# Two transformer blocks: zero matmuls in the plan's gaps, an early table for ScalarE, a new model of the DMA limits and new offsets

## The chip, the cores and the metric

The kernel runs on one core of a Trainium2 chip. The time is device microseconds of one execution; the number given is the median of the runs. TensorE (PE) multiplies, and its weight loads are listed apart (PEld); VectorE (DVE), ScalarE (ACT) and GpSimd (POOL) do the rest; SyncE (SP) only issues DMAs.

## What is computed

256 tokens of width 1024 go through two blocks of two layers each. In every layer of the first block there is a feed-forward (ffn1), a mixer of a bidirectional gated DeltaNet and a Hyena of order 2 (mix1), and a second feed-forward (ffn2). In every layer of the second block there is a mixer of differential attention, retention and a short convolution with gates (mix2), and a feed-forward with a convolution (ffn3). Cut to its frame:

```python
def _swiglu(h, w_gate, w_up, w_down):
    return (jax.nn.silu(h @ w_gate) * (h @ w_up)) @ w_down
for i in range(DEPTH):                                   # first block
    x = x + 0.5 * _swiglu(_rmsnorm(x, ffn1_norm[i]), ...)
    proj = _rmsnorm(x, mix_norm[i]) @ w_in[i]
    x = x + concatenate([o_dn, o_hy], axis=-1) @ w_out[i]   # DeltaNet, Hyena
    x = x + 0.5 * _swiglu(_rmsnorm(x, ffn2_norm[i]), ...)
# Hyena, after a short convolution of u into v, x1, x2
zz = v
for o, gate in enumerate((x1, x2)):
    zz = gate * (_fft_conv(zz, kspec[:, o]) + skip[o] * zz)
# second block, per layer
x = x + (gate0 * (o_da @ w_da) + gate1 * (o_ret @ w_ret) + gate2 * (o_sc @ w_sc)) @ w_out
x = x + (silu(conv(g_ff)) * u_ff) @ w_ffn_out
```

Inputs and outputs are fp32, and the result has to hold to fp32 accuracy.

## The kernel before

**Weights.** All weights come as 604 chunks of 128x1024 fp32 (512 KB), in the order of use, through SP's DMA queue into four buffers `ws`. ScalarE copies each into `wh` (rounded to fp32r, four buffers), and VectorE, sometimes POOL, makes the rest `wl = ws - wh`. The activations are split in the same way. One product is three fp32r matmuls (`mm3`, L689): high by high, low by high, high by low. A chunk of 128x1024 takes 24 matmuls of 128x256. Results gather in PSUM, three banks `mm` (tile names `pmm_...`) and five `acc` (`pacc_...`). What is left in fp32 (transposes, token sums by `cst`, the doubling in the DeltaNet's solver) is multiplied as fp32. In the names, `c_...` is an activation or constant in SBUF, `sm_...` a narrow one, `par` and `cst` the parameters and constants, `ds` and `dv` buffers in DRAM.

**The plan.** The kernel doesn't issue its instructions as they are written. Class `Plan` records every call as an operation with engine, cost, predecessors and tiles (`note`, L396), places all of them on a simulated clock (`place`, L447) and emits them in the order of the planned starts (`emit`, L616; every instruction has the line of `emit`, L621). So each engine's queue is in the order that the plan gives, and the engines wait for each other by semaphores. `place` takes, on an engine that is free, the ready operation of the highest rank; the rank is the length of the work behind it (times `SLACK` outside TensorE's main chain), and the table `AHEAD` adds an offset by kind and part ("mix1 hyena", "sq0"). Operations that may run on VectorE or POOL (`et`, L701) go by the table `POOL`: of a name's operations every n-th goes to POOL. DMAs are held back while the planned bus is more than `BACK` us ahead. After a gap, TensorE's next group is charged up to 1.7 us more for a slow clock.

**The start.** `setup` (L942) issues on ScalarE's queue the four parts of x and `cst`, then `par`; other constants (`hyf`, `feats`, `cdec`, `oh`, `relb`) follow on the same queue from the parts that need them, and the plan mixes them with ScalarE's copies. While ScalarE's next instruction is a DMA that can't be issued yet, the copies behind it wait. ScalarE's function table is loaded ahead of its first activation.

**mix1.** Beside the projections' main chain, side parts run: the DeltaNet's convolution, solver and scan, and `hyena` (L1578). For each of its two orders: sums and differences `c` with transposes, four products with `zmat` (128x512), eight products of the results with the filter's spectrum on VectorE, then `imat` matmuls and the multiplication by the gate (`hg`, may go to POOL).

## Time and profile before

| | us |
|---|---|
| median of the runs | 1942.88 (1941.55 to 1950.27, three runs) |
| the profiled execution | 1946.58 |
| its span, first to last instruction | 1944.9 |
| TensorE busy | 1910.2 (98%) |
| VectorE busy | 1509.2 (78%) |
| ScalarE busy | 1090.5 (56%) |
| POOL busy | 213.1 (11%) |
| mean granted clock of TensorE | 0.994 |

Busy times count instructions, not waits. A busy TensorE can still be slow: at the lower of its two clock levels (1.2 instead of 2.4 GHz, a granted clock of 0.50) a matmul takes about twice as long, so the clock of a stretch is read beside its busy time. "Idle before <-X" names what an instruction waited for. A time stands at the start of a row in us from the start of the span.

### The profile page before, as it was taken

Reading aid. Unit: us, or ns where it says so; the run is one execution under the profiler, and the core shown is the slowest. Engines: PE = TensorE matmul, PEld = TensorE weight load, DVE = VectorE, ACT = ScalarE, POOL = GpSimd, SP = SyncE. Lnnn points to the kernel's source line nnn. Section 1 sums busy time; section 2 is a strip of 40 time slices with the busy share of each in tenths; the row PEclk is TensorE's granted clock in tenths of the full one; section 3 lists DMA queues with packets and bytes.
Section 4 is the critical chain, followed back from the end, with each engine's and each line's share of the span. In section 5 each row is a group of like instructions: output and inputs, shape, how many; then the busy total and the mean of one; then the engine's idle time right before and its main releaser. Section 6 shows DMA issues by size and latency. Waiting matters only on the chain.

```text
span 1944.9 us, 36536 instructions
## 1 busy us (share of the span) xinstructions
PE 1910.2 (98%) x14038; PEld 1800.6 (93%) x14038; DVE 1509.2 (78%) x3067; ACT 1090.5 (56%) x1792; POOL 213.1 (11%) x218
## 2 busy tenths in 40 slices
PE   7999998999999999999999999999999999999999
PEld 7998997999999999998999999999999999999998
DVE  7768879986669667899886679766977788669776
ACT  5656664565556555664555565455655654556564
POOL 0000041000000000222000002233000012240000
PEclk9999998999999999999999999999999999999999
DMA  8655763255555556552565544555555544555553
GB/s 293 212 185 170 230 195 103 91 197 189 184 186 178 189 186 217 201 149 85 166 195 186 189 167 163 180 185 187 183 186 192 174 153 161 191 182 191 188 185 130
DMA packets 127046, 348.84 MB, mean 179 GB/s; under 512 B 24758, under 2 KB 39960, under 8 KB 126872
## 3 DMA queue, kind: packets, MB, share of 16 engines
q1 hardware_dynamic: 115584, 326.89, 51.3%
q10 hardware_dynamic: 11288, 19.63, 2.9%
q8 instruction: 110, 1.80, 0.4%
q14 instruction: 64, 0.52, 0.1%
HBM read 333.61 MB, written 11.81 MB: 178 GB/s over the span
## 4 chain that ended last, share of the span: by engine, by line
PE 91%; DVE 5%; ACT 1%; DMA 1%; issue 1%; ACTq 0%; POOL 0%; SPq 0%; DVEq 0%; POOLq 0%
PE pmm L621 57%; PE pacc L621 35%; DVE c L621 4%; DVE wl L621 1%; ACT c L621 1%; ACTq L621 0%; ACT wh L621 0%; DVE sm L621 0%; DVE x L621 0%; DMA ds<-c 0%; DMA c<-dv 0%; DMA ws<-in_W 0%; DMA x<-in_x 0%; POOL c L621 0%; ACT L621 0%
## 5 line engine op out<-in xcount | busy, mean ns | idle before, releaser
L621 PE MATMUL pmm<-c,wh 128*128 128x256 f32 (+1 forms) x4576 | 1102.4, 322 | 9.9 <-ACT wh L621 8.6
L621 ACT ACTIVATE wh<-ws 128x1024 fp32r<-128x1024 f32 (+1 forms) x604 | 635.6, 1055 | 537.0 <-PE pmm L621 221.3
L621 DVE TENSOR_TENSOR wl<-ws,wh 128x1024 fp32r<-128x1024 f32 (+1 forms) x562 | 687.7, 1226 | 270.9 <-ACT wh L621 265.0
L621 PE MATMUL pmm<-c,wl 128*128 128x256 f32 x3056 | 859.6, 281 | 0.1
L621 PEld LDWEIGHTS pmm<-c,wh 128*128 128x128 f32 x4576 | 759.8, 189 | 81.1 <-ACT wh L621 8.6
L621 PEld LDWEIGHTS pmm<-c,wl 128*128 128x128 f32 x3056 | 577.6, 189 | 1.0 <-DVE wl L621 0.6
L621 PE MATMUL pacc<-c,wh 128*128 128x256 f32 x3136 | 566.9, 281 | 0.0
L621 PEld LDWEIGHTS pacc<-c,wh 128*128 128x128 f32 x3136 | 482.6, 189 | 6.1 <-issue 0.7
L621 PE MATMUL pacc<-c,wl 128*128 128x256 f32 x1568 | 440.5, 281 | 0.0
L621 PEld LDWEIGHTS pacc<-c,wl 128*128 128x128 f32 x1568 | 296.0, 189 | 0.0
L621 ACT ACTIVATE c<-c 128x256 fp32r<-128x256 f32 (+4 forms) x412 | 181.2, 450 | 157.2 <-DVE c L621 144.3
L621 DVE TENSOR_TENSOR c<-c,c 128x256 f32<-128x256 f32 (+7 forms) x345 | 166.9, 497 | 7.9 <-ACT c L621 4.4
L621 DVE TENSOR_TENSOR c<-pmm,c 128x256 f32<-128x256 f32 (+1 forms) x292 | 134.5, 461 | 41.9 <-PE pmm L621 36.0
L621 DVE SCALAR_TENSOR_TENSOR c<-c,c 128x256 f32<-128x256 f32 (+3 forms) x288 | 129.3, 450 | 14.3 <-ACT c L621 7.7
L621 POOL TENSOR_TENSOR wl<-ws,wh 128x1024 fp32r<-128x1024 f32 x42 | 104.2, 2480 | 263.3 <-ACT wh L621 145.0
L621 DVE SCALAR_TENSOR_TENSOR c<-c,par,c 128x256 f32<-128x256 f32 x248 | 114.7, 482 | 22.9 <-ACT c L621 21.7
L621 PE MATMUL pacc<-c,c 128*128 128x128 f32 (+5 forms) x700 | 98.9, 302 | 2.8 <-DVE c L621 1.4
L621 ACT ACTIVATE c<-pacc 128x512 f32<-128x512 f32 (+4 forms) x125 | 59.2, 495 | 64.3 <-PE pacc L621 60.2
L621 POOL TENSOR_TENSOR c<-c,c 128x256 f32<-128x256 f32 (+1 forms) x50 | 60.9, 1222 | 291.6 <-DVE c L621 245.5
L621 PEld LDWEIGHTS pacc<-c,c 128*128 128x128 f32 (+2 forms) x700 | 83.1, 195 | 8.9 <-DVE c L621 2.3
L621 ACT ACTIVATE c<-c,par 128x256 f32<-128x256 f32 x96 | 52.8, 574 | 51.0 <-DVE c L621 50.4
L621 DVE TENSOR_TENSOR c<-pacc,c 128x512 f32<-128x512 f32 (+4 forms) x126 | 72.0, 610 | 9.3 <-PE pacc L621 6.6
(85 smaller groups left out, 997.6 us busy)
## 6 DMA issues: line engine op xcount, KB each, us to landing
ws<-in_W SPq DMA_DIRECT2D x600, 512.0 KB, 3.4
ds<-c ACTq DMA_DIRECT2D x20, 256.0 KB, 4.7
c<-ds ACTq DMA_DIRECT2D x20, 256.0 KB, 3.8
c<-dv SPq DMA_DIRECT2D x32, 128.0 KB, 2.7
dv<-c SPq DMA_DIRECT2D x8, 256.0 KB, 5.0
dg<-c SPq DMA_DIRECT2D x8, 256.0 KB, 3.2
c<-in_cm ACTq DMA_DIRECT2D x6, 256.0 KB, 5.0
ws<-in_W SPq DMA_DIRECT2D x4, 256.0 KB, 6.4
```

Source lines behind the costliest of these rows:

```text
L621: getattr(e, call)(*a, **kw)
```

## The change

Five things change in the plan, and the order of all queues with them.

1. `AHEAD` (the offsets) is new as a whole, `POOL` (what POOL takes) in nine places, `BACK` is 3.0 instead of 5.
2. The plan's limits for DMAs: 330 instead of 360 KB per us; a DMA waits for the end of the eighth before it (`lanes`); a DMA that follows a DMA, issued by ScalarE, is planned 6.5 us after it; an issue holds ScalarE for 0.35 us.
3. A gap on TensorE is charged with up to 0.3 us, not 1.7 (`COLD`).
4. `emit` puts matmuls of zeros into TensorE's queue where the plan has it waiting for more than 0.45 us (`FILL`). They write into the PSUM tile of the group that follows; the group's first matmul starts the tile anew. At the very start they begin at the planned 3.5 us. POOL makes the zeros in `setup`, by a memset and a copy to fp32r.
5. `setup` gives ScalarE a Tanh on two columns, so that the table is loaded early.

There are 74 zero matmuls: 22 of 128x256 ahead of the first real one, 13 of 128x256 soon after, in layer 0 of mix1 four of 128x512, 13 of 128x1 and one of 128x128 in fp32, in layer 1 six of 128x512 and six of 128x128 in fp32, and nine of 128x256 in four other places. ScalarE loads its table 11 times instead of 13.

Between VectorE and POOL: in layer 0 of mix1 two weight subtractions and one `hg` product go from POOL to VectorE, in layer 1 two subtractions, in mix2 eight; 17 other operations go the other way, among them four elementwise products of mix1 and ffn and nine weight subtractions of mix2 and ffn3.

```diff
-BACK = 5
-AHEAD = {' cst': -57, ' prep': 0, ' sq0': 25, ' x0': 82, 'conv': 5, ...
+BACK = 3.0
+AHEAD = {' ': 42.0, ' cst': 51.0, ' prep': -105.0, ' sq0': 391.0, ' table': -150.0, ...
+COLD, FILL = .3, .45
-POOL = {'ba': 1, 'by': 1, 'gate': 4, 'hg': 3, 'ht': 2, 'hx0': 2, 'hx1': 4, 'hx3': 2, 'mask': 1, 'rot': 4, 'rvg': 1, 'sc': 2, 'sc1': 6, 'se': 4, 'v1': 6, 'wo2': 2}
+POOL = {'ba': 4, 'by': 1, 'daq': 4, 'gate': 6, 'hg': 6, 'ht': 2, 'hx0': 2, 'hx1': 4, 'mask': 1, 'rot': 4, 'rqk': 3, 'rvg': 1, 'sc': 2, 'se': 4, 'sh': 4, 'sq': 6, 'wo2': 2}
...
-            return out.shape[0] * n * 4 / 360e3 * (1.0 if n > 300 else 1.6)
+            return out.shape[0] * n * 4 / 330e3 * (1.0 if n > 300 else 1.6)
...
-            return .95
+            return 6.5 if b.dma and b.eng == "ACT" else .95
...
-        hw = bus = 0.0
+        hw, bus = 0.0, 3.0
+        lanes = [0.0] * 8
...
-                    if ops[i].dma and bus > t + BACK:
+                    if ops[i].dma and max(bus - BACK, lanes[-8]) > t:
...
-                    now[e] = t + .06 if e != "POOL" else t + 1.1
+                    now[e] = t + (.06 if e == "SP" else .35)
...
+                    lanes.append(bus + .2)
...
-                        c += 1.7 * min(max(t - now[e] - 1.1, 0.0) / 2.2, 1.0)
+                        c += COLD * min(max(t - now[e] - 1.1, 0.0) / 2.2, 1.0)
...
+        end, pitch = 3.5, .2
...
+            if o.eng == "PE":
+                if o.start - end > FILL:
+                    self.keep_busy(o.calls[0], o.start - end - .2, pitch)
+                end, pitch = o.end, .118
...
+    def keep_busy(self, first, us, pitch):
+
+        call, a, kw = first
+        out = a[0]
+        n = int(np.prod(out.shape[1:]))
+        fast = call == "matmul" and kw["rhs"].dtype == F32R
+        z = self.zero if fast else self.zero32
+        z, w = z[:, 0:n], z[:, 0:out.shape[0]]
+        if len(out.shape) == 3:
+            z = z.rearrange("p (a b) -> p a b", a=out.shape[1])
+        start = True if call == "transpose" else kw["start"]
+        for _ in range(int(us / (pitch * max(1.0, n / (256 if fast else 64))))):
+            self.real["PE"].matmul(out, lhsT=w, rhs=z, start=start, stop=False, skip_group_check=True)
...
+        nc.zero = fix.tile([128, 512], F32R, name="zero")
+        nc.zero32 = fix.tile([128, 512], F32, name="zero32")
+        nc.gpsimd.memset(nc.zero32, 0.0)
+        nc.gpsimd.tensor_copy(out=nc.zero, in_=nc.zero32)
...
-        nc.part = ""
+        nc.part, nc.hold = "table", .35
+        z = self.T("sm", [128, 2, 2])
+        nc.vector.memset(z[:, 0], 0.0)
+        self.act(z[:, 1], z[:, 0], AF.Tanh)
+        nc.part, nc.hold = "", 0.0
```

At three places the order of an engine's queue is shown. In the names the last number counts the kernel's tiles and moves by two or three from before to after, so `wh_127` of before is `wh_130` of after. ScalarE at the start, before, from the split of the first weights to the copy `wh_127`:

```order
L621 ACTIVATE wh_102<-ws_101 128x512
L621 ACTIVATE wh_105<-ws_104 128x512
L621 DMA c_71_154<-in_hyf 64x256
L621 DMA c_70_153<-in_feats 33x256
L621 DMA c_142_225<-in_hyf 128x512
L621 DMA c_134_217<-in_cdec 128x512
L621 DMA c_135_218<-in_cdec 128x512
L621 DMA c_246_330<-in_hyf 128x512
L621 DMA par<-in_par 128x1764
L621 ACTIVATE wh_127<-ws_126 128x1024
L621 DMA c_210_293<-in_oh 32x256
```

And after, over the same work:

```order
L631 ACTIVATE wh_123<-ws_122 128x1024
L631 ACTIVATE wh_105<-ws_104 128x512
L631 ACTIVATE wh_108<-ws_107 128x512
L631 ACTIVATE c_12_92<-x 128x256
L631 ACTIVATE c_13_93<-x 128x256
L631 DMA c_72_157<-in_hyf 64x256
L631 ACTIVATE wh_130<-ws_129 128x1024
L631 DMA c_71_156<-in_feats 33x256
L631 DMA c_143_228<-in_hyf 128x512
L631 DMA par<-in_par 128x1764
L631 ACTIVATE wh_143<-ws_142 128x1024
```

The copy (now `wh_130`) has come ahead of the DMAs of `feats`, `hyf` and `par`, and `cdec`, one `hyf`, `oh` and `relb` have gone further back; `cst`, which was issued in front of all activations, stands three rows above the first one shown.

TensorE in layer 0 of mix1, before: the last transforms by `zmat`, a sum by `cst`, a product of the filter (64x256) and the `imat` matmuls (128x129) of the Hyena; `pacc_824` is the DeltaNet's doubling in fp32:

```order
L621 MATMUL pacc_904<-c_787_871,zmat 128x512
L621 MATMUL pacc_904<-c_788_872,zmat 128x512
L621 MATMUL pacc_904<-c_787_871,zmat 128x512
L621 MATMUL pacc_900<-cst,c_802_886 128x1 x4
L621 MATMUL pacc_1083<-c_981_1065,c_982_1066 64x256
L621 MATMUL pacc_940<-imat,c_802_886 128x129
L621 MATMUL pacc_940<-imat,c_845_929 128x129
L621 MATMUL pacc_940<-imat,c_812_896 128x128
L621 MATMUL pacc_940<-imat,c_843_927 128x128
L621 MATMUL pacc_940<-imat,c_802_886 128x129
L621 MATMUL pacc_940<-imat,c_845_929 128x129
L621 MATMUL pacc_824<-c_700_784,c_660_744 128x2x4x16 x2
```

And after, with the zeros (L645):

```order
L631 MATMUL pacc_883<-c_788_874,zmat 128x512
L631 MATMUL pacc_883<-c_789_875,zmat 128x512
L631 MATMUL pacc_883<-c_788_874,zmat 128x512
L645 MATMUL pacc_907<-zero 128x512
L631 MATMUL pacc_907<-c_788_874,zmat 128x512
L631 MATMUL pacc_907<-c_789_875,zmat 128x512
L631 MATMUL pacc_907<-c_788_874,zmat 128x512
L645 MATMUL pacc_903<-zero_80 128x1 x13
L631 MATMUL pacc_903<-cst,c_803_889 128x1 x4
L631 MATMUL pacc_1086<-c_982_1068,c_983_1069 64x256
L645 MATMUL pacc_827<-zero_80 128x2x4x16
L631 MATMUL pacc_827<-c_701_787,c_661_747 128x2x4x16 x2
```

The doubling (now `pacc_827`) stands ahead of the `imat` matmuls, and 15 zero matmuls fill three gaps here (three more are a few rows earlier).

VectorE in layer 1 of mix1, before: from the second to the fourth product of the Hyena's transforms with the spectrum (`c_2119`, `c_2128`, and then `c_2129`), with the DeltaNet's convolution (`c_1966`, `c_2010`) and weight subtractions (`wl`) between:

```order
L621 TENSOR_TENSOR c_2119_2203<-pacc_2196,c_2116_2200 128x512
L621 SCALAR_TENSOR_TENSOR c_1966_2050<-c_1961_2045,par,c_1966_2050 128x256
L621 TENSOR_TENSOR c_1955_2039<-pacc_2038,c_1925_2009 128x512
L621 TENSOR_TENSOR c_1951_2035<-pacc_2034,c_1898_1982 128x512
L621 SCALAR_TENSOR_TENSOR c_1966_2050<-c_1961_2045,par,c_1966_2050 128x256
L621 SCALAR_TENSOR_TENSOR c_2010_2094<-c_2004_2088,par,c_2010_2094 128x256 x2
L621 SCALAR_TENSOR_TENSOR sm_1993<-sm_1991,sm_1990 128x8
L621 SCALAR_TENSOR_TENSOR c_1966_2050<-c_1967_2051,c_1966_2050 128x512
L621 TENSOR_TENSOR wl_2211<-ws_2209,wh_2210 128x1024
L621 SCALAR_TENSOR_TENSOR c_2010_2094<-c_2011_2095,c_2010_2094 128x512
L621 TENSOR_TENSOR c_2128_2212<-pacc_2193,c_2116_2200 128x512
L621 TENSOR_TENSOR wl_2240<-ws_2238,wh_2239 128x1024
```

And after, from the first of the eight products (`c_2119` here) to the last:

```order
L631 TENSOR_TENSOR c_2119_2205<-pacc_2196,c_2116_2202 128x512
L631 TENSOR_TENSOR c_2120_2206<-pacc_2199,c_2117_2203 128x512
L631 TENSOR_TENSOR c_2129_2215<-pacc_2196,c_2117_2203 128x512
L631 TENSOR_TENSOR c_2130_2216<-pacc_2199,c_2118_2204 128x512
L631 TENSOR_TENSOR c_2160_2246<-pacc_2223,c_2158_2244 128x512
L631 TENSOR_TENSOR c_2161_2247<-pacc_2240,c_2159_2245 128x512
L631 TENSOR_TENSOR c_2162_2248<-pacc_2223,c_2159_2245 128x512
L631 TENSOR_TENSOR c_2163_2249<-pacc_2240,c_2158_2244 128x512
```

The eight products now stand in a row, and the convolution and two weight subtractions have moved behind them.

## Rows read from the trace of the kernel before

**Rows 1.** The page, part 1: engine, busy us (share of the span), instructions.

```profile
PE 1910.2 (98%) x14038; PEld 1800.6 (93%) x14038; DVE 1509.2 (78%) x3067; ACT 1090.5 (56%) x1792; POOL 213.1 (11%) x218
```

**Rows 2.** Windows, long: from:to, length, busy us (x instructions) by engine, clock, DMA share, GB/s.

```profile
350.00:780.00 430.00, 429.73 (x3053) 401.49 (x3052) 324.61 (x588) 237.66 (x380) 11.82 (x13) 1.00 0.55 183
1050.00:1900.00 850.00, 848.74 (x6382) 806.28 (x6381) 646.95 (x1290) 476.63 (x776) 126.35 (x109) 1.00 0.54 180
```

**Rows 3.** Windows of the start.

```profile
8.60:15.00 6.40, 6.30 (x26) 5.76 (x27) 6.37 (x12) 6.40 (x13) 0.00 (x0) 1.00 0.78 281
15.00:20.80 5.80, 5.80 (x51) 5.80 (x51) 2.42 (x6) 1.07 (x2) 0.00 (x0) 1.00 1.02 375
20.80:24.10 3.30, 0.30 (x4) 0.09 (x2) 2.99 (x14) 2.21 (x3) 0.00 (x0) 1.00 1.02 394
24.10:28.60 4.50, 4.50 (x26) 4.50 (x27) 4.21 (x9) 2.82 (x7) 0.94 (x1) 0.62 0.94 313
```

**Rows 4.** Timeline of ScalarE (ACTq issues DMAs): start, length, what, [idle before <-releaser].

```profile
5.28 1.28 ACT L621 ACT_TABLE_LOAD   x1 [5.28 <-DMA x<-in_x]
6.58 1.43 ACT L621 ACTIVATE c<-x 128x512 f32<-128x512 f32 x3
...
14.39 0.62 ACT L621 ACTIVATE wh<-ws 128x512 fp32r<-128x512 f32 x1
18.33 0.33 ACTq L621 DMA_DIRECT2D c<-in_hyf  x1
...
19.20 1.06 ACT L621 ACTIVATE wh<-ws 128x1024 fp32r<-128x1024 f32 x1 [4.19 <-DMA ws<-in_W]
```

**Rows 5.** Timeline of VectorE at the start.

```profile
20.29 1.23 DVE L621 TENSOR_TENSOR wl<-ws,wh 128x1024 fp32r<-128x1024 f32 x1 [3.38 <-ACT wh L621]
...
23.89 0.15 DVE L621 SCALAR_TENSOR_TENSOR sm<-sm,sm 128x2 f32<-128x2 f32 x1
```

**Rows 6.** Timeline of TensorE, at the start and in layer 0 of mix1.

```profile
15.56 0.50 PE L621 MATMUL pacc<-cst,c 128*128 128x1 f32 x4
...
24.10 0.43 PE L621 MATMUL pacc<-cst,sm 128*128 128x128 f32 x2 [3.00 <-DVE sm L621]
...
309.83 1.41 PE L621 MATMUL pacc<-c,zmat 128*128 128x512 f32 x5 [1.23 <-DVE c L621]
```

**Rows 7.** Windows around 220 and 250 us, and of both layers of mix1.

```profile
219.80:223.20 3.40, 3.40 (x18) 3.40 (x17) 3.40 (x13) 0.63 (x1) 0.00 (x0) 0.50 0.48 161
240.00:260.00 20.00, 17.16 (x135) 16.18 (x134) 15.84 (x47) 10.76 (x18) 7.10 (x10) 1.00 0.73 238
303.70:311.90 8.20, 5.16 (x31) 3.57 (x30) 8.15 (x23) 4.36 (x10) 0.00 (x0) 1.00 0.21 25
311.90:318.80 6.90, 3.97 (x12) 2.33 (x12) 6.37 (x11) 0.48 (x2) 2.55 (x2) 0.75 0.75 201
318.80:325.60 6.80, 5.44 (x25) 5.45 (x26) 5.44 (x10) 4.15 (x8) 0.71 (x2) 0.50 0.67 200
...
868.00:875.00 7.00, 5.12 (x37) 4.19 (x35) 6.96 (x19) 5.23 (x13) 0.00 (x0) 1.00 0.31 35
875.00:878.50 3.50, 3.20 (x8) 2.53 (x9) 3.37 (x6) 0.00 (x0) 0.00 (x0) 0.52 0.71 185
878.50:892.00 13.50, 10.36 (x79) 9.16 (x78) 11.95 (x22) 7.66 (x17) 6.45 (x6) 1.00 0.75 228
...
919.50:923.00 3.50, 3.42 (x16) 3.42 (x17) 3.50 (x9) 1.23 (x2) 0.91 (x2) 0.51 0.14 23
```

**Rows 8.** VectorE's groups from 868 to 892: count, busy us, mean ns, idle before.

```profile
L621 DVE SCALAR_TENSOR_TENSOR c<-c,par,c 128x256 f32<-128x256 f32 x15 | 6.7, 479 | 0.0
L621 DVE TENSOR_TENSOR c<-pacc,c 128x512 f32<-128x512 f32 x9 | 6.0, 685 | 0.3 <-PE pacc L621 0.3
L621 DVE TENSOR_TENSOR wl<-ws,wh 128x1024 fp32r<-128x1024 f32 x3 | 3.7, 1249 | 0.0
```

**Rows 9.** The page, part 5: POOL's weight subtractions.

```profile
L621 POOL TENSOR_TENSOR wl<-ws,wh 128x1024 fp32r<-128x1024 f32 x42 | 104.2, 2480 | 263.3 <-ACT wh L621 145.0
```

More of the change, by code (lines that the diff above doesn't have):

```diff
@@ L27 @@
 A3 = (2,)
-BACK = 5
-AHEAD = {' cst': -57, ' prep': 0, ' sq0': 25, ' x0': 82, 'conv': 5, 'cst': -50, 'da': 40, 'decay': 10, 'double': -20, 'ffn1 finish': 60, 'ffn1 norm': 110, 'ffn1 norm0': 5, 'ffn1 prep': 10, 'ffn1 sq': 25, 'ffn2 finish': -4, 'ffn2 prep': 40, 'ffn2 scaled': 0, 'ffn2 spec': 85, 'ffn2 split': 5, 'ffn3 finish': -40, 'ffn3 norm': 0, 'ffn3 prep': 40, 'ffn3 scaled': 42, 'ffn3 split': -7, 'ffn3 sq': 48, 'finish': 82, 'g0': 5, 'hyena': 10, 'kk': -10, 'mix1 double': 30, 'mix1 finish': 83, 'mix1 hyena': 20, 'mix1 kk': 10, 'mix1 out': 78, 'mix1 prep': 38, 'mix1 qk': 66, 'mix1 solve': 20, 'mix1 sq': 32, 'mix1 w': 3, 'mix2 finish': 12, 'mix2 norm': 162, 'mix2 prep': -40, 'mix2 ret': 95, 'mix2 split': -22, 'mix2 sq': 5, 'norm': 153, 'norm0': 152, 'out': 80, 'prep': 10, 'qk': 23, 'ret': 168, 'solve': 10, 'spec': 80, 'split': -2, 'sq': 28, 'sq0': 40, 'w': 8, 'x0': 2}
+BACK = 3.0
+AHEAD = {' ': 42.0, ' cst': 51.0, ' prep': -105.0, ' sq0': 391.0, ' table': -150.0, ' x0': 211.0, 'conv': -109.0, 'cst': -269.0, 'da': 42.0, 'decay': -341.0, 'double': 200.0, 'ffn1 finish': 53.0, 'ffn1 norm': 545.0, 'ffn1 norm0': 357.0, 'ffn1 prep': 21.0, 'ffn1 scaled': -91.0, 'ffn1 spec': 80.0, 'ffn1 split': -2.0, 'ffn1 sq': 317.0, 'ffn2 ': -7.0, 'ffn2 finish': 264.0, 'ffn2 norm': 277.0, 'ffn2 prep': 356.0, 'ffn2 scaled': -74.0, 'ffn2 spec': 71.0, 'ffn2 split': 20.0, 'ffn2 sq': 255.0, 'ffn3 ': -7.0, 'ffn3 finish': -9.0, 'ffn3 norm': 347.0, 'ffn3 prep': 138.0, 'ffn3 scaled': 87.0, 'ffn3 split': -108.0, 'ffn3 sq': -123.0, 'finish': 190.0, 'hyena': 30.0, 'kk': 85.0, 'mix1 ': -1.0, 'mix1 conv': 5.0, 'mix1 decay': 19.0, 'mix1 double': 290.0, 'mix1 finish': -416.0, 'mix1 hyena': 14.0, 'mix1 kk': 6.0, 'mix1 norm': 198.0, 'mix1 out': 51.0, 'mix1 prep': -14.0, 'mix1 qk': 252.0, 'mix1 solve': 213.0, 'mix1 split': -2.0, 'mix1 sq': -91.0, 'mix1 w': 5.0, 'mix2 da': 39.0, 'mix2 finish': 9.0, 'mix2 norm': 155.0, 'mix2 prep': -134.0, 'mix2 ret': 227.0, 'mix2 split': -279.0, 'mix2 sq': 47.0, 'norm': 395.0, 'norm0': -167.0, 'out': 258.0, 'prep': -248.0, 'qk': 386.0, 'ret': 113.0, 'scaled': -259.0, 'solve': 107.0, 'spec': 56.0, 'split': -14.0, 'sq': 206.0, 'sq0': -116.0, 'table': 56.0, 'w': 54.0, 'x0': 205.0}
 WIN = 1500
 LOCK = True
+COLD, FILL = .3, .45
 RG = 2
-SLACK = 2
+SLACK = 2.0
 HEAD = 2
@@ L540, in place @@
                         continue
-                    if ops[i].dma and bus > t + BACK:
+                    if ops[i].dma and max(bus - BACK, lanes[-8]) > t:
                         skip.append((r, i))
-                        heapq.heappush(events, bus - BACK)
+                        heapq.heappush(events, max(bus - BACK, lanes[-8]))
                         continue
@@ L617, in emit @@
         ops = self.ops
+        end, pitch = 3.5, .2
         for i in sorted(range(len(ops)), key=lambda i: (ops[i].start, i)):
-            e = self.real[ops[i].eng]
-            for call, a, kw in ops[i].calls:
-                getattr(e, call)(*a, **kw)
+            o = ops[i]
+            e = self.real[o.eng]
+            if o.eng == "PE":
+                if o.start - end > FILL:
+                    self.keep_busy(o.calls[0], o.start - end - .2, pitch)
+                end, pitch = o.end, .118
+            for call, a, kw in o.calls:
+                getattr(e, call)(*a, **kw)
+    def keep_busy(self, first, us, pitch):
[10 more added lines that the diff above has]
+            self.real["PE"].matmul(out, lhsT=w, rhs=z, start=start, stop=False, skip_group_check=True)
 class Build:
```

## The prediction

> **What bounds the kernel now.** I read the page first. TensorE is busy for 1910.2 us, 98% of the span [rows 1], so all waits together are 35 us, and the question is only where these lie and which of them the new plan takes away. Windows over long stretches come next: from 350 to 780 us TensorE works 429.73 of 430.00 us and from 1050 to 1900 it works 848.74 of 850.00, both at a granted clock of 1.00 [rows 2]. There is nothing to win there, and something to lose. What can be won lies at the start, around 250 us, and in the two layers of mix1 (303 to 326 and 868 to 923 us).
>
> At the start three things cost time. ScalarE waits until 5.28 us for x, and only then loads its table (1.28 us); its first activation starts at 6.58 [rows 4]. Until 15.0 us the matmuls run slowly: 26 in 6.30 us, 0.242 each, and from then 51 in 5.80 us, 0.114 each [rows 3]. (The clock is written as 1.00 in both rows; the pace says half.) Then, between 15.0 and 18.33 us, ScalarE does nothing: two DMA issues stand in its queue ahead of `wh_127`, and the copy starts at 19.20 us after an idle 4.19 [rows 4]. VectorE has waited 3.38 us for it with the subtraction `wl_128` when that starts at 20.29, and the chain for the reciprocal root, which stands behind it, ends at 23.89 [rows 5]. TensorE meets this at the matmul of `cst` and `sm`, which starts at 24.10 after 3.00 us of waiting [rows 6], and in the 4.50 us behind it the granted clock is 0.62 [rows 3].
>
> In mix1 the hyena chain bounds. From 303.7 to 311.9 us TensorE works 5.16 of 8.20 us and VectorE 8.15; then 3.97 and 6.37 of 6.90, then 5.44 of 6.80 at clock 0.50 [rows 7]. So VectorE is the engine that others wait for, TensorE is idle for 3.04 + 2.93 + 1.36 = 7.3 us, and the clock falls for it. In layer 1 TensorE is idle for 1.88 us (868 to 875), 0.30 and 3.14 us (878.5 to 892), again beside a VectorE that is nearly full [rows 7].
>
> **The start, -6.0 us (-2.5 to -8.4).** (a) The table: the early Tanh on two columns brings the load behind the first DMA of x, into a time in which ScalarE does nothing. Once x is there ScalarE can begin 1.30 us earlier. But the other three DMAs of x stand behind the load in its queue, so they are issued about 1.3 us later, and `cst` much later. Between 0 and 1.3; I take 1.0, since the first matmul needs only the first slice. The Trainium skill (*ScalarE: Activation LUTs*, section *What ACT_TABLE_LOAD costs*) gives 1283 ns for the load and some 1380 ns of draining, 2.66 us in all. The trace has 5.28 + 1.28 = 6.56 and the next activation at 6.58 [rows 4]: no drain is seen, and by the page's figure this part would be 2.4 and the sum 1.4 us better. (b) 22 zero matmuls of 128x256 now run ahead of the first real one; at 0.242 they last 5.3 us, within the 8.6 us in which TensorE waits, so they cost nothing by themselves. The zeros are made by a memset and a copy on POOL, which is free then. If the full pace comes about 5 us earlier, 20 of the 26 slow matmuls gain 0.128 each: 2.6. A faster TensorE then runs into weights that are not there (DMA share 0.78 and 1.02 [rows 3]), so 1.0 of 0 to 2.6. (c) The queue: the order shows `wh_130` (the former `wh_127`) ahead of all but one of the DMAs that stood before it (`cst` has come in front), and the first `spread` matmul a few groups later. The 3.00 us go, unless the late `cst` or the full DMA queues give a new wait; 1.0 to 3.0, taken 2.5. (d) With the wait goes the slow stretch behind it, 0.38 of 4.50 = 1.7; 0 to 1.5 of it, taken 1.5. Together 6.0.
>
> **The stretch from 240 to 260 us, -2.0 (0 to -2.8).** TensorE works 17.16 of 20.00 us [rows 7]. The new order puts 66 more matmuls ahead of the longest of the three waiting groups (7.5 us at 0.114), so that wait is covered; the other two move less.
>
> **Layer 0 of mix1, -5.0 (-1 to -11).** At most all the idleness goes, 7.3, and what the low clock costs, 0.25 x 3.97 + 0.50 x 5.44 = 3.7. Against it stands VectorE, which bounds: between the start of the chain and its end it has 77 instructions instead of 81. At the mean of 0.49 us (1509.2 by 3067 [rows 1]) that is 2.0 us. The `hg` product that POOL did, and that now is VectorE's, is among the 77. Independent TensorE work also moved: the fp32 doubling (`pacc_824`) now stands ahead of the transforms, where TensorE waited before. I take 2.5 of the idle 7.3 and 2.5 of the 3.7, for 18 zeros stand in the gaps: 4 of 128x512 at 0.28 [rows 6], 13 of 128x1 at 0.125 [rows 6] and one more, 3.0 us in all, inside gaps of 7.3.
>
> **Layer 1 of mix1, -4.0 (0 to -8.5).** Here the order of VectorE is plainly better: before, nine rows of other work stand between the second and the third product of the chain and two more before the fifth (two weight subtractions of 1.249 us, five scalar_tensor_tensor of 0.479, two evictions of 0.685 [rows 8] and two more of that size, 7.6 us), and after, all eight products follow each other. The chain ends up to 7.6 us earlier; what it can free is the idle 1.88 + 0.30 + 3.14 = 5.3 us, and the low clock, 0.48 x 3.20 + 0.49 x 3.42 = 3.2 [rows 7]. What was pushed behind is late next (the convolution of the DeltaNet and its triangular solve), so I take half.
>
> **Other edits.** The slow stretch at 219.8 us costs 0.50 x 3.40 = 1.7 [rows 7]; two zeros stand ahead of it, and I take -0.5 (0 to -1.7). The 52 zeros that are not at the very start would cost, all in front of work that is ready, 13 x 0.242 + 9 x 0.114 + 10 x 0.28 + 13 x 0.125 + 7 x 0.28 (the 128x128 in fp32, priced by the widest) = 10.6 us. They are placed where the plan has a gap, the trace has most of those gaps, and I take +1.0. New offsets for every kind of work also make new waits: the stretches in rows 2 can only lose. Twenty-odd operations changed between VectorE and POOL, a weight subtraction costing 1.249 on one [rows 8] and 2.48 on the other [rows 9]; both engines have room there, so +2.0 (0 to +6). The limit on DMAs only delays issues and SP's queue has no other work; it counts among these 2 us.
>
> **The sum.** -6.0 - 2.0 - 5.0 - 4.0 - 0.5 + 1.0 + 2.0 = -14.5 us. The profiled execution took 1946.58 us, 1.7 more than its span and 3.7 over the median of the runs, 1942.88. So 1946.6 - 14.5 = 1932.1 for such an execution and 1928.4 on the scale of the median; I say 1928. About a third of the sum is the clock. The Trainium skill (*TensorE: Matmul & The Clock Gate*, Part 1) says of modelling that the ramp costs under 1% of a typical span and is not to be fitted. The rows give 13.6 us for all seven slow stretches, 0.7%, so the rule holds in size, but here it is as large as the whole question; with it left out the sum would be -9.
>
> **Rivals.**
> - *VectorE stays the bound.* TensorE's idleness in mix1 is VectorE's fullness (8.15 of 8.20 us [rows 7]); a new order of the same work moves the waits without removing them. Then the start (-6), half of the stretch at 250 (-1), zeros and new waits (+3): -4, or 1939. For it speaks that layer 0 loses only four instructions; against it the rows of layer 1.
> - *The change doesn't do what it says:* the zeros are too few, 3.0 us in gaps of 7.3, the clock falls as before, and only waits go: -4.5 - 2 - 2.5 - 2.5 + 1 + 2 = -8.5, or 1934.
> - *Everything holds:* -8.4 - 2.8 - 11 - 7 - 1.7 + 1 = -30, or 1913. It needs VectorE's chain to be short enough twice.
> - *Slower: the work taken from POOL lands on the full VectorE.* In each layer of mix1 two subtractions come from POOL (2 x 1.249), in layer 0 an `hg` product (0.685, as an eviction of its size) too: +3.2 and +2.5 on the chain that TensorE waits for, and what waits there is colder; the eight in mix2 add up to 10 us to an engine 76% busy (646.95 of 850 [rows 2]), of which 4 may show; zeros that stand in front of ready work add 7.5, if the chain's lateness is elsewhere than planned. +17, less what the start still gives (-6): +11, or 1954. It decides if the chain comes later than in the trace of before, by more than the gaps hold.
>
> **How the numbers follow.** The forecast has a chance of 0.53, VectorE as the bound 0.17, the clock that falls anyway 0.12, everything holds 0.12, slower 0.06. A measurement of this kernel tells about 0.5% from no change, 9.7 us: faster is below 1933.2, slower above 1952.6. Faster: 0.50 of the forecast, all of "everything", 0.05 and 0.03 of the two others, 0.70; slower 0.06; the rest, 0.24, is within. The range of 8 in 10 reaches to the best case and over the first two rivals: 1914 to 1940.
>
> **What would show it.** In the profile after: the table load before 3 us and the first activation at about 5.3; full pace from about 10 us; no wait over 1 us at the `spread` matmul; clock 1.00 behind it. At 240 to 260 us TensorE busy for over 19 of 20. In layer 0 the rows from 303 to 326 with 2 to 3 us less idleness and no stretch at 0.50; in layer 1 the eight products back to back and TensorE's idleness at about 2.5. The long stretches of rows 2 should still be full. I am wrong if TensorE waits at the start for `cst` or for weights, if the zeros are followed at once by work that had long been ready, or if waits turn up between 1050 and 1900 us.

## The result, and the profile after

The changed kernel takes 1925.88 us (median; 1923.87 to 1926.70, four runs) against 1945.37 us for the kernel before, measured again beside it. The ratio is 0.990, with an interval of 0.987 to 0.992: 19.5 us less. On the page of its profile (span, busy times, granted clock of 40 slices):

```profile
span 1925.0 us, 36646 instructions
...
PE 1911.6 (99%) x14132; PEld 1805.0 (94%) x14132; DVE 1511.1 (78%) x3065; ACT 1086.5 (56%) x1791; POOL 214.7 (11%) x223
...
PEclk9999998999999999999999999999999999999999
```

TensorE's busy time has hardly moved, 1911.6 against 1910.2 [rows 1], but 18.6 us of it are zeros (the sum of their groups). The real matmuls take 1893 us, 17 less, in part since more of them ran at full pace; and TensorE is idle for 13.4 us where it was for 34.7. The waits of TensorE that are left (in total, times, longest):

```profile
PE pacc L631 <- DVE c L631: 2.9, 6, 1.1
PE pmm L645 <- POOL zero L631: 2.6, 1, 2.6
PE pacc L631 <- ACT c L631: 1.0, 3, 0.4
PE pmm L631 <- DVE wl L631: 0.9, 1, 0.9
```

In the same view of before, matmuls into `pacc` waited 8.6 us for `c` from VectorE and 6.2 for `c` from ScalarE; that has fallen to 2.9 and 1.0. By stretch, before (from:to, length, busy us (x instructions) of PE, PEld, DVE, ACT, POOL, then clock, DMA share, GB/s), the start, the stretch around 250 us and the two layers of mix1:

```profile
0.00:50.00 50.00, 38.32 (x279) 37.05 (x280) 35.48 (x73) 27.29 (x46) 3.91 (x12) 0.97 0.86 297
215.00:270.00 55.00, 52.16 (x391) 49.36 (x390) 44.09 (x126) 31.19 (x50) 12.58 (x15) 0.97 0.68 222
290.00:335.00 45.00, 37.59 (x258) 33.86 (x258) 40.76 (x108) 17.96 (x33) 9.58 (x10) 0.89 0.40 113
...
840.00:930.00 90.00, 83.85 (x650) 79.57 (x649) 85.89 (x229) 47.41 (x89) 19.43 (x19) 0.96 0.40 115
```

And after, over the same work, with the second block's row, which answers to [rows 2]:

```profile
0.00:45.00 45.00, 40.85 (x314) 39.94 (x315) 33.42 (x66) 27.53 (x45) 6.27 (x15) 1.00 0.87 302
210.00:261.00 51.00, 51.00 (x404) 49.26 (x403) 46.44 (x128) 31.97 (x51) 11.98 (x14) 1.00 0.66 230
281.00:324.00 43.00, 40.70 (x275) 36.70 (x274) 36.45 (x102) 18.21 (x34) 7.62 (x9) 0.88 0.33 93
...
827.00:912.00 85.00, 82.85 (x667) 79.01 (x666) 83.38 (x215) 45.70 (x85) 16.98 (x18) 1.00 0.36 107
...
1050.00:1900.00 850.00, 849.98 (x6400) 807.42 (x6399) 654.07 (x1296) 478.27 (x779) 132.55 (x111) 1.00 0.53 180
```

The stretch around 250 us is full, layer 1 nearly so, and the second block has lost its last idle 1.2 us. Layer 0 (281 to 324) still has a clock of 0.88.

Windows count a zero as work and a waiting matmul as busy. So I also worked out from the records of TensorE what each stretch loses: its length, less every real matmul that starts in it at the steady pitch of its shape (the 40th percentile of the distance to the next one, in before). Idleness, low clock and zeros are all in it:

| us lost | before | after | no zeros | without the narrow zeros | wide zeros |
|---|---|---|---|---|---|
| start (50 us of before) | 17.1 | 12.4 | 11.7 | 11.7 | 12.3 |
| of it, the first 20 us | 12.0 | 11.8 | 11.5 | 11.5 | 11.8 |
| 215 to 270 | 6.3 | 1.2 | 0.8 | 1.1 | 1.1 |
| layer 0 of mix1 | 13.4 | 13.0 | 10.6 | 9.3 | 7.9 |
| 580 to 620 and 780 to 800 | 3.9 | 0.7 | 0.8 | 1.1 | 1.0 |
| layer 1 of mix1 | 12.5 | 7.5 | 7.8 | 7.3 | 8.3 |
| 1150 to 1260 (mix2) | 8.5 | 7.0 | 6.6 | 7.2 | 7.1 |
| median of the runs | 1945.4 | 1925.9 | 1924.1 | 1922.0 | 1922.1 |

Each column is one execution, and the clock alone can differ between two executions by some 2 us in one stretch (below). The execution of after (1926.70 us) is the slowest of its four, that without zeros (1922.85) the fastest of its five. Of the places listed, layer 0 is the one where nothing was won. And of the 4.7 us that the start gives, all but 0.2 lie behind the first 20 us.

### The profile page after: what moved, and what is told of

The parts are those of the page before. It is cut to its first block, busy times and chain, and to the rows that moved or that the text cites. A ratio compares the mean times of both kernels' runs of the same rounds, so it can differ in the third digit from the quotient of the medians.

```text
span 1925.0 us, 36646 instructions
## 1 busy us (share of the span) xinstructions
PE 1911.6 (99%) x14132; PEld 1805.0 (94%) x14132; DVE 1511.1 (78%) x3065; ACT 1086.5 (56%) x1791; POOL 214.7 (11%) x223
## 4 chain that ended last, share of the span: by engine, by line
PE 77%; DVE 4%; issue 1%; DMA 1%; ACT 1%; DVEq 0%; ACTq 0%; SPq 0%
PE pmm L631 49%; PE pacc L631 28%; DVE c L631 4%; DMA ws<-in_W 1%; DVE wl L631 0%; ACT c L631 0%; ACT wh L631 0%; DVE x L631 0%; DVE sm L631 0%; PE pacc L645 0%; PE pmm L645 0%; DVEq L631 0%; ACT sm L631 0%; ACTq L631 0%; SPq L631 0%
## 5 line engine op out<-in xcount | busy, mean ns | idle before, releaser
L631 DVE TENSOR_TENSOR c<-c,c 128x256 fp32r<-128x256 f32 (+9 forms) x339 | 160.0, 485 | 6.8 <-ACT c L631 2.9
L631 POOL TENSOR_TENSOR c<-c,c 128x256 f32<-128x256 f32 (+2 forms) x56 | 67.6, 1211 | 583.7 <-DVE c L631 310.7
L631 POOL TENSOR_TENSOR wl<-ws,wh 128x1024 fp32r<-128x1024 f32 x39 | 96.2, 2471 | 208.1 <-ACT wh L631 174.9
```

Of the source, the lines that this page charges most:

```text
L631: getattr(e, call)(*a, **kw)
```

## The experiments

The median of before was 1943.5 to 1945.7 us in the different sets of runs; each kernel below was run four times or more, and its verdict goes by the median beside after's 1925.9 or beside before in the same set.

### No zeros at all

```diff
-                if o.start - end > FILL:
+                if False:
```

> The changed kernel with no zero matmul at all, every other instruction in its place. After shows 1925.9 us. Theory A (the zeros pay for themselves by the clock): at the start the full pace comes some 6.4 us after the first real matmul, as in before, so near 13.9 us instead of 8.4 (+1 to +3); the slow stretch near 215 us comes back (+1.7), those of layer 1 too (+1.5 to +3.2); in layer 0 the 26 narrow records that took 4.2 us are gone (-2 to -3): 1928 to 1931 in all. Theory B (the order alone made the gain, the zeros are at best neutral): 1922 to 1926, and the clock falls in the same places as before.

Measured: 1924.09 us (1922.85 to 1925.39). Theory B by the time: without a single zero the kernel is no slower than after (1.8 us less, with overlapping ranges), and 21.5 us faster than before in the same set. In the profiled execution the clock does better than B asked: it falls in layer 0 only. At 215 us the new order has no wait that would need filling. In layer 1 it has one of 2.2 us, and the clock stays up all the same. But this is the fastest of the five executions, with a mean granted clock of 0.998; the other four have 0.995 to 0.996, so in them the clock fell for longer or in other places too; where is not recorded. At the start the first real matmul comes earlier than in after (7.47 us), since no zeros stand before it:

```profile
6.57 0.79 PE L631 MATMUL pmm<-c,wh 128*128 128x256 f32 x2 [6.57 <-ACT wh L631]
```

### Zeros at the start alone

```diff
-                if o.start - end > FILL:
+                if o.start - end > FILL and end == 3.5:
```

> The changed kernel with the 22 zeros ahead of the first real matmul and no others. If the start is where zeros pay, it keeps full pace from about 8.4 us, and against the kernel without zeros it is 1 to 3 us faster. If the first 15 us are set by the arrival of x and weights, both take the same time within 0.7. Against after it has the clock's falls near 215 us and in layer 1 back (+3 to +5) and the narrow zeros of layer 0 gone (-2 to -3): 1925 to 1929.

Measured: 1924.63 us (1923.91 to 1925.79), the same as without any, and a little below the range expected against after. The start is not set by TensorE's pace but by what arrives: after runs at full pace from 8.4 us and the kernel without zeros from 13.4, and by 20 us they have lost 11.8 and 11.5. With the zeros at the start alone the clock rose at 7.3 us in the profiled execution, and fell again at 14.2 us behind the wait that the 13 other zeros fill in after; 14.5 us were lost up to 45 us, 11.7 without zeros.

### No early table

```diff
             o = ops[i]
+            if o.part == "table":
+                continue
```

> The changed kernel without the early Tanh and its memset; every other instruction in its place, so the table is loaded ahead of the first activation on x. Theory A (the load was on the path): the first activation comes 1.3 us later (6.1 instead of 4.8 us) and the kernel takes 1.0 to 1.3 us more, 1927. Theory B (the first 15 us are set by the other slices of x, which now are issued earlier): the same within 0.5 us.

Measured: 1925.06 us (1924.00 to 1926.36), nothing lost. But the run moves less than theory A says: without the Tanh the table is loaded at 2.69 us, long before x is there, and the first activation on x starts at 5.12 and not at 6.1. ScalarE in this kernel:

```profile
2.69 1.28 ACT L633 ACT_TABLE_LOAD   x1 [2.69 <-issue]
5.12 1.03 ACT L633 ACTIVATE c<-x 128x512 f32<-128x512 f32 x2 [1.14 <-DMA x<-in_x]
```

And in after:

```profile
1.26 1.28 ACT L631 ACT_TABLE_LOAD   x1 [1.26 <-PEq L2132]
1.32 1.34 ACTq L631 DMA_DIRECT2D x<-in_x  x3
...
4.82 1.03 ACT L631 ACTIVATE c<-x 128x512 f32<-128x512 f32 x2 [2.06 <-DMA x<-in_x]
...
14.46 0.33 ACTq L631 DMA_DIRECT2D par<-in_par  x1
...
14.90 1.05 ACT L631 ACTIVATE wh<-ws 128x1024 fp32r<-128x1024 f32 x1
```

The first activation on x starts at 4.82 instead of 6.58 us [rows 4], and par's DMA at 14.46 with the copy `wh_130` right behind it. Of these 1.8 us the Tanh makes only 0.3. The other 1.5 come with the order of the queue: in before the table load stood behind the issue of `cst`, which after issues at 10.78 us. ScalarE in before:

```profile
4.92 0.33 ACTq L621 DMA_DIRECT2D cst<-in_cf  x1
```

On TensorE little follows from the 1.8 us (timeline of after):

```profile
2.62 5.06 PE L645 MATMUL pmm<-zero 128*128 128x256 f32 x22 [2.62 <-POOL zero L631]
7.47 0.63 PE L631 MATMUL pmm<-c,wh 128*128 128x256 f32 x2
...
11.98 1.72 PE L645 MATMUL pmm<-zero 128*128 128x256 f32 x13
...
14.81 0.39 PE L631 MATMUL pmm<-c,wl 128*128 128x256 f32 x1 [0.88 <-DVE wl L631]
```

22 zeros run until 7.47 us, and at 11.98 and 14.81 it waits for the next slices and `wl` all the same. The first real matmul comes 1.1 us earlier than in before (8.58), and by 20 us only 0.2 us of gain are left.

### The DMAs back ahead of the copy at the start

```diff
+        copies = [i for i in order if ops[i].eng == "ACT" and any(self.tag[nm] == "wh" for nm in ops[i].tiles)]
+        at = order.index(copies[5])
+        late = [i for i in order[at:] if ops[i].eng == "ACT" and ops[i].dma][:6]
+        order = order[:at] + late + [i for i in order[at:] if i not in late]
```

> The changed kernel with one thing undone in the queue of ScalarE: the six DMAs that follow wh_130 (feats, two of hyf, par, two of cdec) stand ahead of it again, as in before. Theory A (the order of this queue made the gain at the start, 17.1 to 12.4 us lost in the first 50): wh_130 waits behind them, up to 4 us of ScalarE's time come back, VectorE's root chain and the spread matmul wait again, and the kernel takes 2.5 to 5 us more, 1928 to 1931. Theory B (the gain at the start came from what is loaded less there, or from the order of VectorE): 1925 to 1927.

Measured: 1931.65 us (1930.69 to 1932.15), 5.8 more than after. Theory A, and more than it asked. ScalarE's queue in this kernel:

```profile
14.10 0.90 ACT L636 ACTIVATE c<-x 128x256 fp32r<-128x256 f32 x2
22.29 0.33 ACTq L636 DMA_DIRECT2D c<-in_cdec  x1
...
23.16 1.06 ACT L636 ACTIVATE wh<-ws 128x1024 fp32r<-128x1024 f32 x1 [8.16 <-DMA ws<-in_W]
```

The second `cdec` and a `hyf` wait for the queue, and the copy behind them starts at 23.16 after 8.16 us of idleness, twice that of before [rows 4]. The row names the weights' DMA as what the copy waited for, but in after the same copy ran at 14.90. TensorE meets it as in before, only longer:

```profile
26.18 0.58 PE L636 MATMUL pmm<-c,wh 128*128 128x256 f32 x1 [6.86 <-DVE c L636]
```

### The plan's new limits alone, and the new offsets alone

The first is the kernel before with `BACK`, 330 KB per us, the lag, the lanes, the issue times and a charge of 0.3; the second with the tables `AHEAD` and `POOL` and nothing else.

> The kernel before with the new limits of DMAs, issue times and charge for a gap in the plan, but the old offsets, the old POOL table, no zeros and no early table. Theory A (the plan now knows what stalls ScalarE's queue): most of the gain at the start and that at 245 to 260 us is in it, 1934 to 1938 against 1945.6 before. Theory B (the new offsets made the gain, the limits only delay issues): 1942 to 1947. In the order the eight products of layer 1 stand together with it too; if that is what counts there, layer 1 gains 4 to 5 us of these.

> The kernel before with the new offsets and the new POOL table, but the old limits, no zeros and no early table. Theory A (limits and offsets only work together, since the offsets were chosen for a plan with these limits): 1936 to 1946. Theory B (the offsets are the gain): 1924 to 1928, as the changed kernel without zeros (1924.1). In its order the eight products of layer 1 are interrupted by ten other rows, so layer 1 should lose more than 7.5 us.

Measured: 1947.66 us with the limits alone (ratio to before 1.002, interval 1.001 to 1.003) and 1956.79 with the offsets alone (1.006, 1.0048 to 1.0075). Each half makes the kernel slower; both together, with the early table and without zeros, make it 21.5 us faster. Neither theory gave these numbers: 1947.66 lies just above the range of theory B, and 1956.79 above both ranges of the second run. With the limits alone the stall of ScalarE's queue is gone (0.8 us lost from 20 to 50, 5.1 before), but the old offsets put five activations on x and other DMAs ahead of the first copy, and TensorE starts at 13.48 us with a token sum:

```profile
13.48 1.01 PE L623 MATMUL pacc<-cst,c 128*128 128x1 f32 x4 [13.48 <-DVE c L623]
```

The expectation for layer 1 failed too. The products stand together in this kernel's order, seven of them in one run on VectorE, yet layer 1 still loses 11.2 us (12.5 before) and not 4 to 5 less. TensorE idles there for 7.1 us, at full clock:

```profile
884.04 4.27 DVE L623 TENSOR_TENSOR c<-pacc,c 128x512 f32<-128x512 f32 x7
...
840.00:930.00 90.00, 82.89 (x665) 78.60 (x664) 86.72 (x223) 50.77 (x101) 19.43 (x20) 1.00 0.38 104
```

With the offsets alone layer 0 loses 17.1 us instead of 13.4, and layer 1 17.1 instead of 12.5: there the chain is cut by other work on VectorE, and TensorE waits three times for over 1.5 us, the first time still ahead of the eight products:

```profile
879.51 0.87 PE L621 MATMUL pacc<-cst,c 128*128 128x128 f32 x6 [1.70 <-DVE c L621]
...
890.71 0.66 PE L621 MATMUL pacc<-cst,c 128*128 128x128 f32 x4 [2.24 <-DVE c L621]
...
898.83 0.55 PE L621 MATMUL pacc<-cst,c 1*128 1x1 f32 x4 [2.50 <-ACT c L621]
```

### Zeros alone, in the plan of before

```diff
+                if o.start - end > FILL:
+                    self.keep_busy(o.calls[0], o.start - end - .2, pitch)
```

> The kernel before, with its own plan, and zero matmuls wherever that plan has TensorE waiting for more than 0.45 us: 16 at the start, 6 of 256 columns in the first 50 us, 32 in layer 0 of mix1 (16 of them of 128x1), 17 in layer 1, the others in six places. Theory A (zeros keep the clock up in gaps that stay): the slow stretches, 13.6 us in before, go in part, 1938 to 1943. Theory B (zeros fill gaps but the waits stay, and the narrow ones cost 0.3 us each): no change within 2 us of 1945.6, or slower.

Measured: 1949.81 us (1949.10 to 1951.01), against 1943.5 for before in the same set: 6 us slower. Theory B: in layer 0, 11.0 us of zeros stand in gaps where before idled for 7.3 (the three windows of [rows 7]), among them 16 narrow ones, and it loses 16.6 us instead of 13.4:

```profile
313.07 5.35 PE L642 MATMUL pacc<-zero 128*128 128x1 f32 x32 [0.68 <-DVE c L628]
```

### The narrow zeros: wide ones in their place, and none

In layer 0 after puts 13 zeros of 128x1 in fp32 ahead of four transposes (`pacc_903`), where the plan has a gap of some 1.6 us. TensorE in after:

```profile
302.54 0.86 PE L631 MATMUL pacc<-c,zmat 128*128 128x512 f32 x3
303.79 4.29 PE L645 MATMUL pacc<-zero 128*128 128x1 f32 x26 [0.39 <-DVE c L631]
308.01 0.58 PE L631 MATMUL pacc<-cst,c 1*128 1x1 f32 x4
```

Each leaves two records in the trace, and the 13 take 4.2 us, 0.325 each. That is a mean of two paces: until the clock falls, at 305.4 us, a record takes 0.112 us and a zero 0.224; behind it the zero takes 0.427. What the group behind them needs is the first product that POOL adds, and that was done at 304.56 us:

```profile
303.29 1.27 POOL L631 TENSOR_TENSOR c<-c,c 128x512 f32<-128x512 f32 x1 [11.87 <-DVE c L631]
```

So they stand over 3 us in front of ready work. And the clock falls among them (windows of after, columns as above):

```profile
303.70:305.40 1.70, 1.61 (x15) 1.61 (x15) 1.70 (x4) 0.00 (x0) 1.24 (x2) 0.99 0.88 248
305.40:315.60 10.20, 9.94 (x46) 9.08 (x46) 5.69 (x10) 3.37 (x7) 2.29 (x3) 0.50 0.48 151
```

The fall does not always come among them. In the kernel with work put back in layer 1 (below), which has the same instructions here, the 13 ran at full clock in 3.0 us, and the clock fell just behind them, for 6.8 us:

```profile
306.16 3.06 PE L650 MATMUL pacc<-zero 128*128 128x1 f32 x26 [0.38 <-DVE c L636]
...
309.30:316.10 6.80, 6.54 (x30) 5.70 (x30) 4.07 (x7) 3.36 (x7) 1.40 (x2) 0.50 0.58 179
```

One kernel replaces the zeros ahead of fp32 groups by fp32r ones over the whole bank, as many as fit at 0.235 us:

```diff
+        if not fast and start and out.tensor.name not in self.begun:
+            bank = self.whole[out.tensor.name][:, 0:512]
+            for _ in range(int(us / .236)):
+                self.real["PE"].matmul(bank, lhsT=self.zero[:, 0:128], rhs=self.zero, ...)
+            return
```

> The changed kernel in which the zeros ahead of fp32 groups (13 of 128x1, 7 of 128x128) are fp32r matmuls of 128x512 over the whole bank, in number by their measured 0.235 us: six, one, four, one and one. Theory A: the narrow fp32 zeros were mispriced (two records and 0.325 us each, 4.2 us for 13, in a planned gap of 1.6) and don't hold the clock, which fell to 0.50 from 305.4 to 315.6 us. Then the gap takes 1.4 us and not 4.2, the clock stays at 1.00 there, and the kernel takes 1919 to 1922 us. Theory B (TensorE waits for VectorE's chain at that place, whatever stands in the gap): the group starts at the same 308 us, and only the clock may stay up, 1922 to 1924. Theory C (the clock falls for another reason): 1925 to 1927, with the fall at 305 us as in after.

Another leaves out just the 13:

```diff
+        if n < 16:
+            return
```

> The changed kernel without the 13 zeros of 128x1 in layer 0 of mix1; the other 61 zeros stay. In after the group behind them starts at 308.0 us, without any zeros at 304.3, with six wide ones at 306.1. Theory A (the 13 narrow ones delay ready work by 2.5 to 3.7 us and don't hold the clock): the group starts at about 305 us, layer 0 loses 10 to 10.5 us instead of 13.0, and the kernel takes 1922.5 to 1923.5; the wide zeros then bring 1 us more by the clock. Theory B (another thing than these 13 makes the difference to the kernel with wide zeros, such as the fp32 zeros of layer 1): 1925 to 1926.5.

Measured: 1922.11 us (1921.22 to 1922.97) with wide zeros, 1922.03 (1921.09 to 1923.39) without the narrow ones: both 3.8 us less than after, both outside its range, and the fastest two kernels here. With wide zeros the mean granted clock is 1.00 in all five executions; without the narrow ones it is 0.998 to 0.999, in after 0.997 to 0.998. The transposes start at 304.30 us without any zeros, at 304.04 without the narrow ones, and at 306.06 behind six wide ones:

```profile
304.30 0.40 PE L631 MATMUL pacc<-cst,c 1*128 1x1 f32 x4 [1.44 <-POOL c L631]
```

```profile
304.04 0.40 PE L631 MATMUL pacc<-cst,c 1*128 1x1 f32 x4 [1.21 <-POOL c L631]
```

```profile
304.47 1.66 PE L649 MATMUL pacc<-zero 128*128 128x512 f32 x6 [0.39 <-DVE c L633]
306.06 0.41 PE L633 MATMUL pacc<-cst,c 1*128 1x1 f32 x4
```

Without the narrow zeros this is theory A, a little better than it asked. With wide ones the time lies just above theory A's range, and the clock is as theory A has it,

```profile
304.00:316.00 12.00, 10.89 (x83) 9.56 (x83) 11.06 (x22) 5.32 (x11) 5.52 (x6) 1.00 0.57 167
```

but the start of the group is between A and B, since six wide ones too stand some 1.5 us in front of it. Layer 0 loses 1.4 us less than without the narrow ones (7.9 against 9.3), the start and layer 1 lose 1.6 more in these two executions, and the time is the same.

### Zeros in layer 0 alone

The wide kernel with zeros only between 280 and 330 us of the plan, 2, 5 and 1 in number.

> The changed kernel with zeros in layer 0 of mix1 alone: 2, 5 and 1 of 128x512 over the whole bank (3, 1, 6 and 1 in the kernel with wide zeros), none at the start, near 215 us, in layer 1 or behind. Theory A (only layer 0 has gaps in which zeros pay): layer 0 loses some 7.5 us, as with wide zeros everywhere (7.9, against 10.6 without any and 13.0 in after), and the rest as without zeros: 1920.5 to 1922, against 1922.1 with wide zeros everywhere and 1924.1 with none. Theory B (the difference of 2 us came from the zeros at the start or in layer 1): 1923.5 to 1925.

Measured: 1923.76 us (1923.21 to 1924.95). In layer 0 theory A holds (7.9 us lost, as with wide zeros everywhere). The whole is theory B: in this execution the clock fell once at the start and once in layer 1 (9.5 us lost, 7.8 without zeros and without such a fall). So the zeros elsewhere are worth 1.6 us against this kernel, whose range lies wholly above that with wide zeros everywhere. Without zeros in these places the clock fell there in two of three profiled executions (this one and that with zeros at the start alone); it did not in the five that have them and keep after's order at the start.

### Layer 1: work back between the products

```diff
+        at = max(n for n, i in enumerate(order) if name(i).startswith("c2_2120_")) + 1
+        late = [i for i in order[at:at + 110] if name(i).startswith(("c2_1956_", "c2_1952_", "c2_1967_", "c2_2011_")) and ...]
+        order = order[:at] + late + [i for i in order[at:] if i not in late]
```

> The changed kernel with six rows of VectorE's queue in layer 1 of mix1 moved back to where before has such rows: two evictions of 0.685 us and four scalar_tensor_tensor of 0.479 between the second and the third product of the Hyena chain, 3.3 us together. Theory A (the chain on VectorE is what TensorE waits for there, and the order of the eight products is the gain of layer 1): layer 1 loses 2.5 to 3.5 us more than in after (7.5), 1928.3 to 1929.5 in all. Theory B (TensorE has enough other work in that stretch): 1925 to 1927.

Measured: 1927.07 us (1925.65 to 1928.39), 1.2 more than after and overlapping with its range: less than theory A asks, though on its side. In after the eight products, and one eviction behind them, are one run on VectorE,

```profile
864.61 5.48 DVE L631 TENSOR_TENSOR c<-pacc,c 128x512 f32<-128x512 f32 x9
```

and moving 3.3 us of other work into it costs TensorE 1.65 us of idleness in the window (3.80 instead of 2.15):

```profile
827.00:912.00 85.00, 81.20 (x648) 77.04 (x647) 81.33 (x208) 45.75 (x85) 16.98 (x18) 1.00 0.36 102
```

So about half of what stands in the chain is seen by TensorE in this window. On the scale of losses it is 9.7 us against 7.5, but from 810 to 930 us 9.8 against 8.8, so 1.0 to 2.2 of the 3.3. That layer 1 gains without zeros too shows the same window without any (4.91 idle, while after has 2.15 and 3.46 of zeros), in an execution in which the clock stayed up there:

```profile
827.00:912.00 85.00, 80.09 (x639) 76.04 (x638) 83.04 (x232) 43.86 (x82) 13.06 (x15) 1.00 0.36 103
```

### The old table of what POOL takes

```diff
-POOL = {'ba': 4, 'by': 1, 'daq': 4, 'gate': 6, 'hg': 6, ...
+POOL = {'ba': 1, 'by': 1, 'gate': 4, 'hg': 3, ...
```

This is the kernel without zeros, planned anew with the table of before.

> The changed kernel without zeros and with the table of before of what POOL takes, so that the subtractions and the product that came from POOL to VectorE in mix1 go back, and those that went the other way too; the plan is computed anew with the new offsets. Theory A (the work moved to VectorE burdens its chain): up to 2 us less than without zeros, 1922 to 1924. Theory B (offsets and table were chosen together, and the order falls apart with the other table; the eight products are interrupted by eight rows in it): 1928 to 1940.

Measured: 1952.52 us (1949.87 to 1953.61), 28 more than without zeros. Theory B, and more than it asked. Layer 0 loses 12.7 us and layer 1 11.2 (10.6 and 7.8 without zeros), but most is lost behind layer 0, between 335 and 450 us of before, where 20.0 us are lost, against 2.4 without zeros. TensorE now idles there, and the clock falls:

```profile
374.00:392.00 18.00, 10.09 (x39) 7.44 (x40) 14.42 (x54) 5.28 (x11) 0.00 (x0) 0.53 0.10 30
```

## Why the prediction was right, and where it was not

Forecast were 1928 us and a range of 1914 to 1940; measured were 1925.9. That the two are 2 us apart is partly luck: before, measured again, was 2.5 us slower than the 1942.88 from which the forecast counts, so the change brought 19.5 us and not 14.5. And the sum was that near only because errors of opposite sign met: layer 0 gave almost nothing, and stretches that were to lose gained. On the scale of the losses above, zeros included, step by step:

- **The start, -6.0: measured -4.7.** The step that holds is (c), ScalarE's queue: undone, it costs 5.8 us, more than the whole start gave, since the copy then waits twice as long as in before. With (c) goes the slow stretch of (d). Steps (a) and (b), 1.0 each, bring 0.2 us together up to 20 us: without the early table the time is the same, and 22 zeros at the start change nothing. The prediction named the reason (weights and x that aren't there) and should have taken the lower end of both. Two readings in (a) were wrong: the table load did not need x, and the other DMAs of x were not held up by it (issued from 1.32 to 2.66 us in after; in before the four went out by 2.67).
- **215 to 270 us, -2.0 and -0.5: measured -5.1.** Too small. Not the two zeros ended the slow stretch: it is gone without them too. No wait explains it either, for TensorE had none ahead of it in before (see the last section), so why the clock fell there is open.
- **Layer 0, -5.0: measured -0.3. This step failed.** It priced the 13 narrow zeros at 0.125 us, from a row of four records [rows 6] that are only two matmuls, since one in fp32 leaves two records; and it took them to lie in gaps. They took 0.224 each at full clock and 0.325 in the mean, in front of work that was ready, and the clock fell among them. That is the prediction's own sign of being wrong: zeros followed at once by work that had long been ready. Without these 13 the layer gains 4.1 us in the one execution profiled (2.8 without any zeros), and the kernel 3.8: so the order of layer 0, with the other five zeros, brings most of what was forecast, and the 13 eat it.
- **Layer 1, -4.0: measured -5.0.** The reason, the eight products in a row, is supported but not settled. Putting back 3.3 of the 7.6 us costs 1.2 us with overlapping ranges. Against it stands the kernel with the limits alone: its products stand in a row, and layer 1 gained 1.3 us. So the row of products is not enough by itself; what else the new order changes there was not taken apart. That the prediction took half and came near is luck in part.
- **The zeros, +1.0: measured +1.8** (after against no zeros, with overlapping ranges), of which 3.9 are the narrow ones and -2.1 the 61 others. These are part of the lines above.
- **New waits, +2.0: measured the other way.** 580 to 620 and 780 to 800 gained 3.2 us, 1150 to 1260 gained 1.5. The prediction said that the full stretches could only lose; they held small waits that the new order covers, such as the idle 1.2 us of the second block.

Of the rivals, that the clock falls anyway came true in layer 0, and only there. The slower one did not come; whether what POOL gave up burdens VectorE's chain was not shown, for with the old table the plan as a whole changes and is 28 us slower. What none of them saw is how the parts hang together: limits alone +4, offsets alone +13, zeros alone +6 us, and limits with offsets (and the early table) -21. The offsets were chosen for one plan; with other limits, or another table for POOL, they lost more than they had won.

The words of the change put the zeros first. They are not what made it faster; the order is. With the DMAs back at the start 9.1 us more are lost there, and 5.8 in the time. The profiled execution gives part of the rest back in layer 0, where it loses 11.4 us instead of 13.0, since the clock fell later there and for 6.8 us instead of 10.2; what remains is spread over many stretches. Of the 13.6 us that the prediction puts down to seven slow stretches, the rows shown give 11.9; the seventh begins 1.4 us before the span ends.

## What to carry to other kernels

Filling a wait of TensorE paid here only where the clock would fall and the filler ended before the real work was ready; price the filler by its own records, and prefer the wide form, which held the clock here, over a narrow one that follows the group's shape. In a list-scheduled kernel such as this, rules and offsets are one thing: test a changed rule only with offsets chosen for it, and look first for a DMA issue that blocks the queue of an engine with copies behind it. Where a part of a change can be left out without moving anything else, run that first: it shows in one run which part carries the gain.

## What the runs showed of the hardware

A zero matmul of one column in fp32 takes longer than one of 256 columns in fp32r. It leaves two records of 0.112 us each at full clock, 0.224 in all (in after, from 303.8 us until the clock falls), and a matmul of 256 columns in fp32r takes 0.114 at full pace [rows 3]. So the narrow form was no cheap filler here.

While TensorE worked on such zeros in after, 1.61 of 1.70 us busy, the granted clock went from 0.99 to 0.50 and stayed there for 10.2 us, although TensorE was busy for 9.94 of these. In five profiled kernels narrow zeros stand in layer 0, and in all five the clock fell among them or within 0.5 us behind them, for 6.8 to 10.2 us. With five or six zeros of 512 columns in their place it stayed at 1.00, in both kernels that have them. A busy TensorE without any zeros doesn't hold the clock either in every case: ahead of the slow stretch at 219.8 us [rows 7] TensorE in before was busy for all of 4.80 us:

```profile
215.00:219.80 4.80, 4.80 (x31) 3.83 (x30) 4.76 (x12) 4.37 (x9) 1.38 (x1) 1.00 0.77 247
```

And the same place can differ from one execution to the next. The same instructions in layer 0 had a slow stretch of 10.2 us in after and without the early table, and of 6.8 with the DMAs back and with work put back in layer 1; without zeros there it was 6.8, without the narrow ones 3.4. In layer 1 the clock held without any zeros in one kernel and fell for 3.4 us in two others that had none there.
